# Moving half of the first layer's output projection beside the second attention, and the context rows behind the first feed-forward products

## Chip, cores, metric

One Trainium2 chip, one of its cores. The metric is the device time of one execution in microseconds (us). TensorE (PE) multiplies, VectorE (DVE) and ScalarE (ACT) do the elementwise work, SyncE (SP) issues the large loads from HBM, and all engines run their own instructions in the order in which they were laid down, waiting on one another through semaphores.

## The reference

Two blocks of two layers each on 256 token rows of width 1024. Only the first layer of the first block matters here; its "even mixer" treats the 256 latent rows and 256 context rows together:

```python
h_l = modulate(x_l, sh1_l, sc1_l); h_c = modulate(x_c, sh1_c, sc1_c)
# ya: neighbourhood attention, yb: differential attention, 512 columns each
y_l = concat([merge_heads(ya_l), merge_heads(rms_norm(yb_l, subln) * (1.0 - lam_init))]) @ w_out
x_l = x_l + g1_l * y_l                      # the same for the context rows
h2  = modulate(x_l, sh2_l, sc2_l)           # row norm, scale, shift
x_l = x_l + g2_l * conv_ffn(h2, w_up, conv_w, conv_b, w_down)
```

The six vectors sh1, sc1, g1, sh2, sc2, g2 of each layer come from one product of the conditioning vector with `w_ada` (1024 x 6144).

## The kernel before

Rows lie as four row tiles of 128 (two of the latent rows `xl`, two of context `xc`, together `xs`), each in two halves of 512 columns. Products in full precision are made of three: an operand is split into a rounded part and a remainder (`wh`, `wl` of a weight: ACT's cast in L359, DVE's subtraction in L360), and `mm3` (L381 to L384) adds high x high, high x low, low x high into a PSUM bank. A weight piece of 1 MB is loaded by SP into one of **three** staging tiles `ws` (`wtile`, L271 to L274, with `loads=3`), then split by `wload` into two of four `wh` and two of four `wl`. Loads are issued in program order, and each waits until its staging tile has been read.

The order of work around the change, in the code from L951:

- `weave` runs generators side by side, always the one that is furthest behind for its share. The second attention `da_att` (L909) goes over four row tiles `t`, and in each over four heads: scores (L879), row maximum on DVE (L921), exponential on ACT (L790), the difference of the two softmaxes (L926), four transposes (L781), the copy of these on ACT (L339), the product with the values (L785). A tail per row tile (L935 to L944: square on ACT, a sum and some fifteen tiny DVE instructions, one multiplication) makes `O[t][1]`.
- Beside it runs `ada` (L437) for three pairs: (0,2) gives g1 and sh2, (0,4) gives sc2 and g2, (1,0) belongs to the next layer. Each pair takes eight loads of 1 MB and, for each, four products straight from the staging tile (L445), then a turn of the result (copy, L454) and a small addition.
- Then the way out: `to_feature` (L714) transposes 128 columns of `O` for all four row tiles, `pairs_from` (L579) splits them; `gate` (L501) spreads g1 over 128 rows by products with a diagonal (L512 on DVE, L518 on PE); `lin_tok` (L632) multiplies with `w_out_e`, all four row tiles of one half of the columns at a time over eight pieces of 128 (`k`), into four banks `acc`; `add_gated` (L673) multiplies by the gate and adds to the row tile (L676, L677). The second half's products wait until all its weights are there and go row tile by row tile (`skew`).
- `modulate` (L561) makes the input of the feed-forward: `norm_rows` (squares in L533, a chain of tiny DVE instructions from L535, multiplication in L539), then per 128 columns two transposes (L550), scale and shift (L571 to L574), split (L575, L576). For the latent rows it runs before the last row tiles; for the context rows it is handed to `conv_ffn` as `begin` and woven with the first products of the latent rows (`stream`, 24 products of 256 columns for each of four results).

A scheduler reorders what `weave` and the code lay down, engine by engine, so the built order is finer than the code's.

Of the kernel before, what the change touches and what calls it, by code (L numbers as in the profile page):

```python
# [166 lines left out]
def run(g):  # L167
    for _ in g:
        pass
# [32 lines left out]
def body(tc, A, stop=None):  # L202
# [62 lines left out]
    def bank():  # L265
        return taken("w")
# [233 lines left out]

    def gate(layer, ch, stream, gb, tag="gate"):  # L501

# [5 lines left out]
        for h in range(2):  # L508
# [6 lines left out]
            yield 0.1  # L515
            ps = bank()
            for j in range(2):
# [195 lines left out]

    def to_feature(rows, cols):  # L714

        ps = bank()
        for i, r in enumerate(rows):
            pe.transpose(ps[:, i * 128:(i + 1) * 128], r[:, cols], ident)
        return ps
# [148 lines left out]
    def v_chunk(c0, res):  # L868
        yield from lin_tok(hT, T4, W, c0, 512, KT, collect(res, lambda: own("v")))
# [39 lines left out]
    def da_att(t):  # L909
# [5 lines left out]
        def unit(j):  # L915
# [13 lines left out]
            def second(P):  # L929
# [19 lines left out]
                 qk_chunk(1536, rtab[0], 0.125, gcol[:, 2:3], qB),  # L949
                 v_chunk(2560, vB)), 68))  # L950
    serve(acc=["a"], pt=["b"])  # L951
    weave((chain(*[da_att(t) for t in T4]), 36), (ada((0, 2), (0, 4), (1, 0)), 24))

    g1 = [[], []]
    gt = chain(*[gate(0, 2, i, g1[i], "v") for i in T2])
    banks(acc=4, w=4)
    oT = [[None] * 8, [None] * 8]
    out = [lin_tok(oT, T4, A["w_out_e"], c0, 512, KT, add_gated(xs, [g1[0], g1[0], g1[1], g1[1]], c0, 512), c0 > 0)
           for c0 in (0, 512)]
    for f in range(8):  # L960
        ps = to_feature([O[t][f // 4] for t in T4], slice((f % 4) * 128, (f % 4) * 128 + 128))
        oT[0][f], oT[1][f] = pairs_from(ps, 512, subln if f >= 4 else None)
        next(gt)
        if f > 1:
            next(out[0])
    run(out[0])
    for _ in range(3):
        next(out[1])
    prs = [pair_tiles(512, "qk") for _ in range(KT)]
    hT = ([p[0] for p in prs], [p[1] for p in prs])  # L970
    run(modulate(prs, (xl, 0, 0), mod[0, 3], mod[0, 4], range(KT)))
    run(out[1])

    def conv_ffn(layer, hT, T, xs, beside=(), begin=None, then=None, gate_tag="gate", act_tags=("act",)):
# [34 lines left out]
        for lo, hi in ((0, 12), (12, NHT)):  # L1009
            acts = []  # L1010
            for f0 in range(lo, hi, 2):
                ww = [wcols(A["w_up"][layer], b + f0 * 128) for b in (0, HID)]
                outs = [pair_tiles(T, act_tags[min((f0 - lo + f) // 4, len(act_tags) - 1)]) for f in T2]
                if f0 == 0 and begin:
                    weave((stream(ww, outs, 0), 10), (begin, 8))
                    run(stream(ww, outs, 256))
# [12 lines left out]
            for c0 in (0, 512):  # L1029
# [5 lines left out]
    conv_ffn(0, hT, 512, xs, ((1, 2),),  # L1035
             modulate(prs, (xc, 1, 256), mod[0, 3], mod[0, 4], range(KT)), None, "oa", ("v", "h"))

# [1130 lines left out]
```

## Time and profile before

| | us |
|---|---|
| median of 3 runs | 2036.98 |
| their range | 2036.53 to 2042.06 |
| the profiled execution, its own time | 2039.93 |
| its span | 2038.1 |
| PE busy in it | 1949.2 (96%) |
| DVE, ACT busy | 1375.5 (67%), 1015.2 (50%) |

The stretch of the change runs from the first scores of the second attention (240 us) to the end of the first four results of the feed-forward for the latent rows (408 us): 168 of the 2038 us. Idle time of PE counts there, and time in which PE runs at the lower of its two clock levels; the profile gives the granted clock as a share of full speed, and half is the lower level.

### The profile page before, as it was taken

How to read it: one execution, taken by the hardware profiler on the slowest of the kernel's cores; microseconds unless marked ns; L12 is line 12 of the kernel's file. 1: busy time of each engine (PE TensorE's matmuls, PEld its weight loads, DVE VectorE, ACT ScalarE, POOL GpSimd, SP SyncE). 2: the span in 40 equal slices, each digit the busy share in tenths (PEclk: the TensorE clock that was granted, in tenths of full speed). 3: DMA queues.
4: the chain of work that ended last, by engine and by line, in shares of the span. 5: the costliest groups of instructions: out<-in, count | busy, mean ns of one | idle time of the engine just before them, and what ended most of it. 6: DMA issues, size and time to landing. Idle time of an engine off the chain costs nothing.

```text
span 2038.1 us, 27898 instructions
## 1 busy us (share of the span) xinstructions
PE 1949.2 (96%) x10697; PEld 1579.4 (77%) x10697; DVE 1375.5 (67%) x2559; ACT 1015.2 (50%) x1662; POOL 31.7 (2%) x65
## 2 busy tenths in 40 slices
PE   7999997899999999998999998899999999999998
PEld 2777545787888888667989866698989788888886
DVE  4546355655445549755767677675767799999897
ACT  4433443433323326254645555454544577777775
POOL 1000000000000000000000200000000000000000
PEclk9999998899999999998999998999999999999999
DMA  9222195136322233444554453445565399999996
GB/s 329 85 93 82 75 318 172 63 124 207 104 89 98 74 117 120 150 146 145 167 200 161 142 171 98 128 165 187 166 193 184 132 356 325 339 332 335 330 334 222
DMA packets 220841, 369.67 MB, mean 181 GB/s; under 512 B 7328, under 2 KB 117516, under 8 KB 215580
## 3 DMA queue, kind: packets, MB, share of 16 engines
q1 hardware_dynamic: 218252, 362.06, 52.6%
q0 software_dynamic: 2448, 5.75, 1.0%
q8 instruction: 86, 1.41, 0.3%
q14 instruction: 55, 0.45, 0.1%
HBM read 366.73 MB, written 1.05 MB: 180 GB/s over the span
## 4 chain that ended last, share of the span: by engine, by line
PE 88%; DVE 5%; ACT 3%; DMA 2%; issue 1%; SPq 0%; ACTq 0%; DVEq 0%
PE w L382 16%; PE w L383 16%; PE w L384 16%; PE acc L384 6%; PE acc L382 6%; PE acc L383 6%; PE ob L785 2%; PE w L879 2%; PE a L382 2%; PE a L384 1%; PE a L383 1%; PE b L382 1%; PE b L384 1%; PE b L383 1%; PE a L445 1%
## 5 line engine op out<-in xcount | busy, mean ns | idle before, releaser
L360 DVE TENSOR_TENSOR wl<-ws,wh 128x1024 fp32r<-128x1024 f32 (+3 forms) x600 | 691.5, 1171 | 251.2 <-ACT wh L359 245.6
L359 ACT CAST wh<-ws 128x1024 fp32r<-128x1024 f32 (+3 forms) x600 | 594.5, 1008 | 377.0 <-PE acc L384 157.3
L382 PE MATMUL w<-h,wh 128*128 128x256 f32 x992 | 283.8, 287 | 2.8 <-DVE raw L1791 1.4
L383 PE MATMUL w<-h,wh 128*128 128x256 f32 x992 | 283.6, 287 | 0.0
L384 PE MATMUL w<-h,wl 128*128 128x256 f32 x992 | 282.2, 285 | 0.5 <-DVE wl L360 0.5
L382 PEld LDWEIGHTS w<-h,wh 128*128 128x128 f32 x992 | 192.5, 194 | 9.7 <-DVE raw L1791 1.6
L384 PEld LDWEIGHTS w<-h,wl 128*128 128x128 f32 x992 | 192.4, 194 | 1.5 <-DVE wl L360 0.7
L383 PEld LDWEIGHTS w<-h,wh 128*128 128x128 f32 x992 | 192.6, 194 | 1.1 <-issue 0.7
L382 PE MATMUL w<-qk,wh 128*128 128x512 f32 (+1 forms) x384 | 146.0, 380 | 0.9 <-ACT t L574 0.9
L383 PE MATMUL w<-qk,wh 128*128 128x512 f32 (+1 forms) x384 | 143.8, 375 | 2.1 <-DVE qk L576 2.1
L383 PE MATMUL w<-wl,h 128*128 128x512 f32 (+1 forms) x384 | 145.1, 378 | 0.7 <-DVE wl L378 0.6
L382 PE MATMUL w<-wh,h 128*128 128x512 f32 (+1 forms) x384 | 144.4, 377 | 0.1
L384 PE MATMUL w<-qk,wl 128*128 128x512 f32 (+1 forms) x384 | 144.3, 376 | 0.0
L384 PE MATMUL w<-wh,h 128*128 128x512 f32 (+1 forms) x384 | 143.7, 374 | 0.0
L382 PE MATMUL acc<-wh,h 128*128 128x512 f32 x272 | 110.0, 405 | 4.0 <-ACT h L583 4.0
L384 PE MATMUL acc<-wh,h 128*128 128x512 f32 x272 | 108.2, 398 | 2.6 <-DVE h L584 2.6
L383 PE MATMUL acc<-wl,h 128*128 128x512 f32 x272 | 107.6, 396 | 0.0
L382 PEld LDWEIGHTS w<-qk,wh 128*128 128x128 f32 x384 | 73.0, 190 | 20.3 <-issue 3.4
L790 ACT ACTIVATE P<-w,s 128x512 f32<-128x512 f32 (+1 forms) x80 | 48.3, 605 | 78.8 <-DVE s L921 28.9
L383 PEld LDWEIGHTS w<-qk,wh 128*128 128x128 f32 x384 | 73.1, 190 | 15.8 <-DVE qk L576 2.6
L383 PEld LDWEIGHTS w<-wl,h 128*128 128x128 f32 x384 | 72.4, 189 | 15.7 <-DVE wl L360 3.8
L384 PEld LDWEIGHTS w<-qk,wl 128*128 128x128 f32 x384 | 73.0, 190 | 13.7
(508 smaller groups left out, 3570.5 us busy)
## 6 DMA issues: line engine op xcount, KB each, us to landing
ws<-in_w_up_dram SPq DMA_DIRECT2D x44, 1024.0 KB, 5.1
ws<-in_w_ada_dram SPq DMA_DIRECT2D x40, 1024.0 KB, 5.0
ws<-in_m_gate_dram SPq DMA_DIRECT2D x32, 1024.0 KB, 6.5
ws<-in_m_up_dram SPq DMA_DIRECT2D x32, 1024.0 KB, 7.8
ws<-in_m_down_dram SPq DMA_DIRECT2D x32, 1024.0 KB, 6.8
ws<-in_w_down_dram SPq DMA_DIRECT2D x20, 1024.0 KB, 5.1
ws<-in_w_in_e_dram SPq DMA_DIRECT2D x12, 1024.0 KB, 5.2
ws<-in_od_w_in_dram SPq DMA_DIRECT2D x12, 1024.0 KB, 5.6
```

Source lines behind the costliest of these rows:

```text
L359: act.copy(wh, ws[:, k:k + e])
L360: split = vec.tensor_tensor(wl, ws[:, k:k + e], wh.bitcast(F32), op=OP.subtract)
L382: pe.matmul(out, lhsT=ah, rhs=bh, start=start, stop=False)
L383: pe.matmul(out, lhsT=ah, rhs=bl, start=False, stop=False)
L384: pe.matmul(out, lhsT=al, rhs=bh, start=False, stop=stop)
L445: pe.matmul(acc[32 * j:32 * j + 32, :], lhsT=cs[:, k, :], rhs=w, start=start, stop=stop)
L785: pe.matmul(ps, lhsT=pts[:, j * 128:(j + 1) * 128], rhs=vs[j][:, vcols], start=first and j == 0, stop=j == n // 128 - 1)
L790: act.activation(P[:, :n], S, AF.Exp, bias=nmax, scale=scale, accum_out=total)
L879: pe.matmul(S[:, :n], lhsT=q[po:po + 64, t * 128:(t + 1) * 128], rhs=k[po:po + 64, 512 - n:512], start=True, stop=True)
```

## The change

- `beside_da` replaces the bare `ada` calls beside the second attention. It runs ada (0,2), then transposes the first four column pieces of the first attention's output (`way_out`), makes all gates, then multiplies them with the upper half of `w_out_e` (`out_rows`: four `k`, one row tile and one half of the columns at a time, added to the rows at once): four row tiles with columns 0 to 511, ada (0,4), four row tiles with columns 512 to 1023, ada (1,0). Inside the last ada it loads the lower half of `w_out_e` (`Wo`).
- After the attention come the four other transposes, the two latent row tiles, `modulate` of the latent rows, the two context row tiles.
- Context's `norm_rows` moves into `begin` (`begin_context`), whose weight in the weave grows from 8 to 12.
- PSUM keeps its division of the attention (`a`, `b` two banks each, `w` three, `ob` one) up to the end of the feed-forward, instead of four `acc` and four `w`.

Every row of `xs` is now added to twice per half of the columns (16 pairs of L676 and L677 instead of 8); matmuls, loads and their sizes are the same.

```diff
+    def out_weights(k0, c0):
+        return wload(A["w_out_e"][k0 * 128:(k0 + 4) * 128, c0:c0 + 512].rearrange("(a p) n -> p a n", p=128), 4, 512)
+    def out_rows(t, k0, c0, wb):
+        ps = bank_a()
+        for k in range(4):
+            c = slice(t * 128, (t + 1) * 128)
+            mm3(ps, oT[0][k0 + k][:, c], oT[1][k0 + k][:, c], wb[k][0], wb[k][1], k == 0, k == 3)
+        add_gated(xs, [g1[0], g1[0], g1[1], g1[1]], c0, 512)(t, t, ps)
+    def beside_da():
+        yield from ada((0, 2))
+        for f in range(4):
+            way_out(f, bank_a)
+            yield 0.5
+        for i in T2:
+            yield from gate(0, 2, i, g1[i], "v", bank_a)
+        for c0 in (0, 512):
+            wb = out_weights(0, c0)
+            for t in T4:
+                out_rows(t, 0, c0, wb)
+                yield 2.7
+            if c0 == 0:
+                yield from ada((0, 4))
+        last = ada((1, 0))
+        for i in range(9):
+            if i in (4, 6):
+                Wo.append(out_weights(4, 512 * (i == 6)))
+            yield next(last)
+        yield from last
+
     serve(acc=["a"], pt=["b"])
-    weave((chain(*[da_att(t) for t in T4]), 36), (ada((0, 2), (0, 4), (1, 0)), 24))
...
-    banks(acc=4, w=4)
...
-    for f in range(8):
-        ps = to_feature([O[t][f // 4] for t in T4], slice((f % 4) * 128, (f % 4) * 128 + 128))
-        oT[0][f], oT[1][f] = pairs_from(ps, 512, subln if f >= 4 else None)
-        next(gt)
-        if f > 1:
-            next(out[0])
-    run(out[0])
-    for _ in range(3):
-        next(out[1])
+    weave((chain(*[da_att(t) for t in T4]), 36), (beside_da(), 51))
+    serve(acc=["a", "b"], w=["w", "w", "w", "ob"], pt=["w"])
+    for f in range(4, 8):
+        way_out(f, bank)
     prs = [pair_tiles(512, "qk") for _ in range(KT)]
     hT = ([p[0] for p in prs], [p[1] for p in prs])
-    run(modulate(prs, (xl, 0, 0), mod[0, 3], mod[0, 4], range(KT)))
-    run(out[1])
+    for i, ts in enumerate((T2, (2, 3))):
+        for c0 in (0, 512):
+            for t in ts:
+                out_rows(t, 4, c0, Wo[c0 // 512])
+        if i == 0:
+            run(modulate(prs, (xl, 0, 0), mod[0, 3], mod[0, 4], range(KT)))
+    def begin_context():
+        xn = norm_rows(xc)
+        yield 4
+        yield from modulate(prs, (xn, 1, 256), mod[0, 3], mod[0, 4], range(KT))
```

How the built order moves, at three places. First SP's queue at the end of the attention (`ada` loads, `w_out_e` loads, then the first of `w_up`), before:

```order
L273 DMA ws_638_2595<-in_w_ada_dram 128x2048
L273 DMA ws_648_2624<-in_w_ada_dram 128x2048
L273 DMA ws_693_2755<-in_w_out_e_dram 128x4x512
L273 DMA ws_720_2871<-in_w_out_e_dram 128x4x512
L273 DMA ws_738_2959<-in_w_out_e_dram 128x4x512
L273 DMA ws_743_2969<-in_w_out_e_dram 128x4x512
L273 DMA ws_792_3189<-in_w_up_dram 128x8x256
```

and after:

```order
L273 DMA ws_695_2812<-in_w_ada_dram 128x2048
L273 DMA ws_703_2834<-in_w_out_e_dram 128x4x512
L273 DMA ws_708_2844<-in_w_ada_dram 128x2048
L273 DMA ws_711_2857<-in_w_ada_dram 128x2048
L273 DMA ws_712_2863<-in_w_out_e_dram 128x4x512
L273 DMA ws_717_2873<-in_w_ada_dram 128x2048
L273 DMA ws_725_2895<-in_w_ada_dram 128x2048
L273 DMA ws_807_3217<-in_w_up_dram 128x8x256
```

The `w_out_e` loads now stand between those of ada; the two before these (one for each half of the columns) stand after the eighth and the sixteenth ada load. On PE the products of the last two loads before (`a` is ada's bank, then its turn L454 and the first transposes of the way out):

```order
L785 MATMUL ob_620_2554<-v_446_1989,pt_663_2674 128x128
L445 MATMUL a_558_2358<-ws_638_2595,cs_95 32x512 x4
L785 MATMUL ob_620_2554<-v_447_1991,pt_663_2674 128x128
L445 MATMUL a_558_2358<-ws_648_2624,cs_95 32x512 x4
L454 MATMUL w_661_2662<-ident_89,t_651_2637 128x128 x4
L718 MATMUL w_672_2707<-ident_89,oa_258_1285 128x128
```

and after:

```order
L785 MATMUL ob_672_2751<-v_447_1991,pt_730_2913 128x128
L445 MATMUL a_682_2770<-ws_708_2844,cs_95 32x512 x4
L445 MATMUL a_682_2770<-ws_711_2857,cs_95 32x512 x4
L445 MATMUL a_682_2770<-ws_717_2873,cs_95 32x512 x4
L445 MATMUL a_682_2770<-ws_725_2895,cs_95 32x512 x4
L454 MATMUL w_738_2942<-ident_89,t_728_2908 128x128 x4
L718 MATMUL w_739_2951<-ident_89,h_551_2327 128x128
```

The last four ada products now stand alone behind all of the attention's. Second, DVE where the gates are made (`dg` diagonals for the gates, `v` the gates themselves, `s` and `P` the attention's softmax and tail, `wl` remainders of `w_out_e`), before:

```order
L512 TENSOR_TENSOR dg_678_2722<-ident_89,s_676_2717 128x512
L940 TENSOR_TENSOR s_665_2679<-s_665_2679,s_664_2678 128x4
L512 TENSOR_TENSOR dg_687_2747<-ident_89,gh_675_2716 128x512
L392 TENSOR_SCALAR s_667_2686<-s_665_2679 128x4
L512 TENSOR_TENSOR dg_688_2749<-ident_89,s_676_2717 128x512
L393 TENSOR_SCALAR s_668_2687<-s_667_2686 128x4
L360 TENSOR_TENSOR wl_695_2758<-ws_693_2755,wh_694_2757 128x1024
```

and after:

```order
L512 TENSOR_TENSOR dg_517_2206<-ident_89,gh_515_2202 128x512
L926 SCALAR_TENSOR_TENSOR P_493_2141<-P_495_2145,s_496_2147,P_493_2141 128x512
L512 TENSOR_TENSOR dg_518_2208<-ident_89,s_516_2203 128x512
L921 TENSOR_REDUCE s_523_2219<-w_521_2215 128x1
L343 COPY v_520_2213<-a_519_2210 128x512
L921 TENSOR_REDUCE s_525_2223<-w_522_2217 128x1
L512 TENSOR_TENSOR dg_528_2231<-ident_89,gh_515_2202 128x512
L512 TENSOR_TENSOR dg_529_2233<-ident_89,s_516_2203 128x512
L924 RECIPROCAL s_527_2227<-s_456_2013 128x1
L360 TENSOR_TENSOR wl_534_2243<-ws_532_2240,wh_533_2242 128x1024
```

All eight diagonals, with the attention's work between them, now stand ahead of the remainder that the first row tile needs; before, four of them did. Third, DVE where the context rows end and their norm begins (`xc` the rows, `s_822` and `s_807` the sums of squares, `qk` the latent rows' last pieces of `modulate`), before:

```order
L676 TENSOR_TENSOR t_790_3157<-acc_736_2957,v_729_2905 128x512
L576 TENSOR_TENSOR qk_765_3072<-t_789_3153,qk_764_3071 128x256
L677 TENSOR_TENSOR xc01_86<-xc01_86,t_790_3157 128x512
L676 TENSOR_TENSOR t_791_3184<-acc_737_2958,v_729_2905 128x512
L677 TENSOR_TENSOR xc11_88<-xc11_88,t_791_3184 128x512
L535 TENSOR_TENSOR s_807_3238<-s_807_3238 128x2
```

and after:

```order
L676 TENSOR_TENSOR t_800_3164<-a_799_3151,v_520_2213 128x512
L576 TENSOR_TENSOR qk_766_3002<-t_798_3147,qk_765_3001 128x256
L677 TENSOR_TENSOR xc00_85<-xc00_85,t_800_3164 128x512
L676 TENSOR_TENSOR t_802_3180<-b_801_3167,v_520_2213 128x512
L676 TENSOR_TENSOR t_804_3196<-a_803_3183,v_531_2238 128x512
L677 TENSOR_TENSOR xc10_87<-xc10_87,t_802_3180 128x512
L677 TENSOR_TENSOR xc01_86<-xc01_86,t_804_3196 128x512
L676 TENSOR_TENSOR t_806_3212<-b_805_3199,v_531_2238 128x512
L677 TENSOR_TENSOR xc11_88<-xc11_88,t_806_3212 128x512
L535 TENSOR_TENSOR s_822_3266<-s_822_3266 128x2
```

All four context pieces are now added behind the last piece of the latent rows, where two were before.

## Rows read from the trace of the kernel before

**Rows 1.** The page's first part: busy time of each engine in the span.

```profile
PE 1949.2 (96%) x10697; PEld 1579.4 (77%) x10697; DVE 1375.5 (67%) x2559; ACT 1015.2 (50%) x1662; POOL 31.7 (2%) x65
```

**Rows 2.** Stretches: us, busy PE, PEld, DVE, ACT, POOL, then PEclk, DMA share, GB/s.

```profile
240.00:408.00 168.00, 144.44 (x802) 93.47 (x801) 101.86 (x282) 67.53 (x155) 0.00 (x0) 0.94 0.54 190
...
250.00:260.00 10.00, 10.00 (x56) 4.26 (x48) 5.15 (x13) 3.75 (x10) 0.00 (x0) 1.00 0.99 366
...
280.00:290.00 10.00, 7.17 (x56) 3.23 (x54) 2.29 (x6) 2.78 (x8) 0.00 (x0) 1.00 0.89 311
...
320.00:330.00 10.00, 3.40 (x10) 2.17 (x11) 9.83 (x25) 3.98 (x6) 0.00 (x0) 0.72 0.80 283
...
380.00:390.00 10.00, 4.63 (x28) 3.74 (x26) 8.90 (x22) 5.58 (x13) 0.00 (x0) 0.79 0.63 210
390.00:400.00 10.00, 8.00 (x49) 7.64 (x50) 5.18 (x16) 3.09 (x7) 0.00 (x0) 0.70 0.00 1
```

**Rows 3.** PE in order of time: start, us, line, tile, count, idle before.

```profile
286.73 1.06 PE L445 MATMUL a<-ws,cs 128*32 128x512 f32 x8 [0.97 <-DMA ws<-in_w_ada_dram]
...
315.93 1.06 PE L445 MATMUL a<-ws,cs 128*32 128x512 f32 x8 [1.03 <-DMA ws<-in_w_ada_dram]
...
324.83 0.79 PE L382 MATMUL acc<-wh,h 128*128 128x512 f32 x1 [4.00 <-ACT h L583]
...
328.65 0.80 PE L384 MATMUL acc<-wh,h 128*128 128x512 f32 x1 [2.60 <-DVE h L584]
...
334.96 0.40 PE L383 MATMUL acc<-wl,h 128*128 128x512 f32 x1
335.19 0.40 PE L384 MATMUL acc<-wh,h 128*128 128x512 f32 x1
```

**Rows 4.** PE in order of time around the context rows' norm.

```profile
384.19 0.39 PE L383 MATMUL w<-qk,wh 128*128 128x256 f32 x1 [1.32 <-DVE qk L576]
...
391.57 1.21 PE L550 MATMUL w<-ident,raw 128*128 128x128 f32 x4 [4.87 <-DVE raw L539]
...
398.02 0.39 PE L382 MATMUL w<-qk,wh 128*128 128x256 f32 x1 [0.44 <-ACT t L574]
...
407.90 0.38 PE L383 MATMUL w<-qk,wh 128*128 128x256 f32 x1
```

**Rows 5.** The tile `in_w_ada_dram`, 236 to 330 us: issues, and time to landing.

```profile
L273 SPq DMA_DIRECT2D ws<-in_w_ada_dram x21: 327/328/331, 244.3 to 308.0; - x21
...
DMA to landing us min/median/max: 4.8/6.9/7.9
```

**Rows 6.** The chain of waits: start, us, engine, tile, line (x2 = one score).

```profile
240.07 1.05 PE w L879 x2
...
249.53 1.00 PE a L445 x8
...
255.08 1.09 PE ob L785 x8
...
297.18 0.62 PE w L879 x2
```

**Rows 7.** Groups by shape, 318 to 410 us: count, busy us, mean ns.

```profile
L360 DVE TENSOR_TENSOR wl<-ws,wh 128x1024 fp32r<-128x1024 f32 x12 | 14.6, 1223 | 7.8 <-ACT wh L359 7.8
...
L359 ACT CAST wh<-ws 128x1024 fp32r<-128x1024 f32 x13 | 13.4, 1046 | 14.4 <-PE acc L384 11.4 <-DMA ws<-in_w_out_e_dram 2.2 <-PE w L383 0.7
```

**Rows 8.** DVE in order of time: start, us; instructions that follow without a wait.

```profile
327.91 0.68 DVE L584 TENSOR_TENSOR h<-w,h 128x512 fp32r<-128x512 f32 x1
328.51 0.68 DVE L512 TENSOR_TENSOR dg<-ident,gh 128x512 fp32r<-128x512 f32 x1
```

**Rows 9.** DVE in order of time: the last attention tail, the context's norm.

```profile
318.18 0.69 DVE L938 TENSOR_REDUCE s<-t 128x4 f32<-128x512 f32 x1 [6.42 <-ACT t L937]
...
388.57 0.16 DVE L535 TENSOR_TENSOR s<-s 128x2 f32<-128x2 f32 x1 [0.79 <-ACT raw L533]
...
390.94 1.67 DVE L539 TENSOR_SCALAR raw<-xc,s 128x512 f32<-128x512 f32 x4
```

More of the change, by code (lines that the diff above doesn't have):

```diff
@@ L499, in ada, with gate @@
         finish(*late)
-    def gate(layer, ch, stream, gb, tag="gate"):
+    def gate(layer, ch, stream, gb, tag="gate", new=bank):
         m = mod[layer, ch][:, :, stream]
@@ L515, in gate @@
             yield 0.1
-            ps = bank()
+            ps = new()
             for j in range(2):
@@ L712, in rope_pairs, with to_feature @@
         vec.tensor_tensor(rv, rv, av, op=OP.add)
-    def to_feature(rows, cols):
-        ps = bank()
+    def to_feature(rows, cols, new=bank):
+        ps = new()
         for i, r in enumerate(rows):
@@ L950, in body @@
                  v_chunk(2560, vB)), 68))
-    serve(acc=["a"], pt=["b"])
-    weave((chain(*[da_att(t) for t in T4]), 36), (ada((0, 2), (0, 4), (1, 0)), 24))
-    g1 = [[], []]
-    gt = chain(*[gate(0, 2, i, g1[i], "v") for i in T2])
-    banks(acc=4, w=4)
-    oT = [[None] * 8, [None] * 8]
-    out = [lin_tok(oT, T4, A["w_out_e"], c0, 512, KT, add_gated(xs, [g1[0], g1[0], g1[1], g1[1]], c0, 512), c0 > 0)
-           for c0 in (0, 512)]
-    for f in range(8):
-        ps = to_feature([O[t][f // 4] for t in T4], slice((f % 4) * 128, (f % 4) * 128 + 128))
-        oT[0][f], oT[1][f] = pairs_from(ps, 512, subln if f >= 4 else None)
-        next(gt)
-        if f > 1:
-            next(out[0])
@@ L966, in body, with way_out @@
-    run(out[0])
-    for _ in range(3):
-        next(out[1])
+    g1 = [[], []]
+    oT = [[None] * 8, [None] * 8]
+    Wo = []
+    def way_out(f, new):
+        ps = to_feature([O[t][f // 4] for t in T4], slice((f % 4) * 128, (f % 4) * 128 + 128), new)
+        oT[0][f], oT[1][f] = pairs_from(ps, 512, subln if f >= 4 else None)
+    def out_weights(k0, c0):
[6 more added lines that the diff above has]
+        add_gated(xs, [g1[0], g1[0], g1[1], g1[1]], c0, 512)(t, t, ps)
@@ L1014, in conv_ffn @@
                 if f0 == 0 and begin:
-                    weave((stream(ww, outs, 0), 10), (begin, 8))
+                    weave((stream(ww, outs, 0), 10), (begin, 12))
                     run(stream(ww, outs, 256))
@@ L1035, in body @@
     conv_ffn(0, hT, 512, xs, ((1, 2),),
-             modulate(prs, (xc, 1, 256), mod[0, 3], mod[0, 4], range(KT)), None, "oa", ("v", "h"))
+             begin_context(), None, "oa", ("v", "h"))
     if stop == "L0":
```

## The prediction

> **What bounds the kernel now.** I read the page's busy shares first: PE works in 96% of the span, no other engine in more than 67% [rows 1]. So only time that PE loses can be won. I then read the stretches from 240 to 408 us, the one in which the change moves work, and PE in order of time there. In these 168 us PE is busy for 144.4, at a mean granted clock of 0.94 [rows 2], so it is idle for 23.6 us, and at the lower level (1.2 of 2.4 GHz) the clock costs some 6 us more: the stretches that start at 320, 380 and 390 us show 0.72, 0.79 and 0.70 [rows 2]. The losses are of three kinds. Up to 317 us ada's loads keep the DMA engines at a share of 0.89 to 0.99, and late in it PE waits for them [rows 2, 3]. Behind the attention PE waits 4.00 and 2.60 us for the first pairs, and runs slowly up to about 334; at 334.96 it is at full speed again, 0.23 us from product to product [rows 3]. Then it waits 1.32 and 4.87 us for the end of the latent rows' `modulate` and for the context rows' norm [rows 4]. The most that can be won is thus about 29 us, 1.4%.
>
> **Prices.** A score of 512 columns takes 1.05 us and one of 256 columns 0.62, eight ada products (one load) 1.00, a set of value products 1.09 [rows 6]; a row tile of `out_rows` is 12 products of 0.23 = 2.76 [rows 3], a result of `stream` 24 products of half that length, 2.8. The split of a weight piece is two casts of 1.05 on ACT and two subtractions of 1.22 on DVE [rows 7]; DVE's instructions of 512 columns, the diagonals among them, are 0.68 long and follow each other in 0.60 [rows 8]. A load takes 4.8 us to land at best, 6.9 in the median [rows 5]; with the queue full it is 1.05 MB / 366 GB/s = 2.87 us from one to the next [rows 2].
>
> **The change, stretch by stretch.** PE's matmuls are the same, so I lay the new orders out over the old prices. Each stretch ends at the point that I name, and its length is PE's work there or the wait that ends later.
>
> (a) 240 us to the end of the first ada set. Three loads are there, five more follow from 244.3 on [rows 5], each when a staging tile is free, so the eighth lands at about 259.3, and its products end at 260.4. PE has about 18 of these 20.4 us to do; the transposes of the first four column pieces fit in, and wait for nothing else.
>
> (b) To the end of the first four row tiles: 27.6 us. The gates now lie on the path. DVE has eight diagonals, two evacuations and five attention instructions ahead of the first remainder, 15 x 0.60 plus 1.4 for tiny ones, and then the remainder's 1.22: with ada's turn (1.3) and 0.5 for waits on PE's scores this is 13.4 us until the second product of the first row tile can run. PE has 10 to 12 us of scores and gate products in that time. Then come 4 x 2.76 and 3.2 of attention.
>
> (c) The second ada set: 19.5 us. Three loads are waiting, five are issued as the products free the tiles; PE's work (8 x 1.00, four scores at 1.05, four sets of values, transposes) is 18.4, and the loads at 2.87 come out about 1 us later.
>
> (d) To the end of the second four row tiles: 22.3 us. The `w_out_e` piece is issued behind the five loads, lands when the set ends, and its split ends 2 us after PE has done three scores; then 17.4 of PE's work.
>
> (e) The third ada set: 26 us, against 14.3 of PE's work. Three of its eight ada loads have landed; the other five and two of `w_out_e` are still to come: seven loads that nothing could issue earlier, since only three staging tiles exist and PE read none of them during (d). The first lands 1.5 + 4.8 after the start, six more at 2.87 each, then 1.06 of products: 24.6. One of them comes about 1.4 later, since its tile is freed by a split that stands behind the last softmax on ACT and DVE: 26. The DMA engines meanwhile stand idle in (b) and (d), for about 20 and 10 us; that is where the time of (e) comes from.
>
> (f) To the first product of the lower half: 6.4 us. ACT's square of the last tail stands behind ada's last copy, so the tail still starts when ada ends: copy and square 1.2, the sum 0.69 [rows 9], 14 tiny instructions at 0.2 = 2.8, the multiplication 0.69, transpose and cast 0.9. Before, the same took 7.8 us from 316.99 to the first product, and 11.7 to the steady run at 328.65 [rows 3], because DVE did four remainders and the diagonals in between.
>
> (g) The eight row tiles of the lower half and the latent rows' 16 transposes: 22.1 + 1.8, plus 2.8 for the low clock after the idle time (as before: 5.5 us of steady work at half speed, 328.65 to about 334) and 0.4: 27.0.
>
> (h) To the context rows' first transpose: 12.4 us. PE has 5.6 us of products (48). DVE first ends the latent rows' last piece, whose scale on ACT waits for two casts that need the last `wh`, then the context rows' seven additions (7 x 0.65), ACT squares, the tiny chain takes 390.94 - 388.57 = 2.4 [rows 9]. PE is idle for about 6.8 us, where it waited 4.87 [rows 4]: the wait that the change means to hide is not hidden, since the first two results only last 5.6 us and the next two stand behind the transposes.
>
> (i) To the end of the latent rows' four results: 10.4 us, two results (5.6), 16 transposes (1.8), low clock (2.2), two waits like the 0.44 for a bank [rows 4].
>
> The sum: 20.4 + 27.6 + 19.5 + 22.3 + 26 + 6.4 + 27.0 + 12.4 + 10.4 = 172.0, against 168 (240 to 407.9 [rows 2, 4]). Behind it nothing moves. So the change costs 4 us: 2043.9 against the profiled execution's own 2039.93, and 2041 against the median of 2036.98, which lies 3 us below that execution. About 0.3% (6.1 us) is what a measurement of this kernel can tell from no change.
>
> Bounds of what the trace does not show. (e) is 24.6 us if no load waits for a split; at the pace of all 21 issues, (308.0 - 244.3) / 20 = 3.19 [rows 5], it is 28, and at the 311 GB/s of 280 to 290 us (3.37 a load [rows 2]) 29. I take the 366 GB/s row, which is the one with a full queue. (b) is 25 if DVE's diagonals slip between the softmax, and 30 if PE's sparse work there costs the clock. (d) is 21 to 25 for the same two reasons, (h) is 9 if DVE adds the context rows ahead of the last piece, 14 if ACT is late. PSUM's new division and the doubled additions lie beside PE's row tiles, which take four times as long, except in (h), where they are counted.
>
> Of the clock the trace shows both: between 280 and 290 us PE is busy for 7.17 of 10 and the granted clock stays at 1.00; after the 4 us of idle time behind 320 it has fallen [rows 2, 3]. The Trainium skill (TensorE: Matmul & The Clock Gate, "HAM oscillation") warns of matmul batches that each wait for a DMA, since each batch then runs cold; (e) is such a loop. By that rule its last products would take 2 us instead of 1; by the row at 280 us they would not.
>
> **Rivals.** *PE stays the bound* (faster). If loads land in time for (c) to (e), because tiles come free in the gaps of PE's order, (e) is its 14.3 us of work, and the sum falls by 11.7 to 160.3: 2029. For it speaks that PE's idle time before was small while loads took 3.2 us each; against it that the last four ada products stand in a row behind everything. It decides if the fourth load of (e) is issued before (d) ends. The Trainium skill (Perfetto Trace Analysis, "Optimization Strategy") advises to interleave regimes with different limits, which would give this result; the old stretch does so already.
>
> *Loads are as slow as before, and the clock falls* (slower). If loads take 3.2 to 3.4 us each, the pace of all issues and of the row at 280 us [rows 2, 5], (a), (c) and (e) grow by 1.5, 2 and 2 to 3, and with PE busy for half of (b) and (e) the first row tiles of each half run at the lower level, 2 us each: 6 to 10 on top of 4, 2047 to 2051. It decides from 3.2 us a load on.
>
> *The change hides what it says* (faster by a little): the context norm ends before the first two results do; (h) is 5.6 and (i) loses its 2.2: 163, or 2032. DVE's order speaks against it.
>
> **Chances.** The sum as worked, within 6 us of no change: 0.45. PE stays the bound: 0.10. The hidden norm: 0.10, half of it (with a shorter (e)) beyond 0.3%. The slow loads and the clock: 0.35, taken as beyond 0.3% since some of it comes on top of the 4 us already. So faster 0.15, same 0.50, slower 0.35. The likeliest is 2041; the range from 2031 to 2051 takes in the bounds of (b), (d), (e) and (h) and most of the slow case, and leaves out PE as the bound.
>
> **What would show it.** In the changed profile: DMA at a low share for some 20 us in the first row tiles and 10 in the second; L445 waiting for `ws` behind the last value products; the stretch from the last score to the first lower product over 15 us; DVE's diagonals ahead of L360 with PE waiting; L550 waiting for `raw` about 7 us. I am wrong if the DMA share stays above 0.8 through the attention, or if PE's order has other gaps than these.

## The result

The changed kernel takes 2057.86 us (2050.36 to 2063.15) where the kernel before takes 2036.76: slower by a factor of 1.0094 (1.0077 to 1.011). A second set of runs gave 2058.72 beside 2039.19, 1.0099 (1.0078 to 1.012). The prediction was 2041, its range ended at 2051. Its nine runs lie in two groups, 2050.4 to 2052.9 (two) and 2057.0 to 2063.2 (seven); the first profile is of a run of 2050.36, a second one, called "again" below, of 2056.99, and what lies between the two is shown there.

First the profile of 2050.36, against the profiled execution of before, 2039.93. Stretches (us, busy time of PE, PEld, DVE, ACT, POOL, then granted clock, DMA share, GB/s): of the kernel before from 240 us to the start of the context rows' first feed-forward result, then of the changed kernel to the same instruction, and 10-us stretches of it.

```profile
240.00:405.18 165.18, 141.62 (x780) 90.83 (x779) 99.46 (x276) 65.85 (x151) 0.00 (x0) 0.94 0.55 193
```

```profile
240.00:416.20 176.20, 147.09 (x779) 90.94 (x778) 110.86 (x292) 65.57 (x152) 0.00 (x0) 0.92 0.50 181
...
270.00:280.00 10.00, 9.75 (x41) 6.70 (x42) 8.85 (x17) 3.80 (x10) 0.00 (x0) 1.00 0.31 107
280.00:290.00 10.00, 10.00 (x49) 6.80 (x48) 8.84 (x28) 3.23 (x7) 0.00 (x0) 1.00 0.00 0
...
320.00:330.00 10.00, 10.00 (x47) 6.71 (x46) 8.43 (x32) 3.12 (x12) 0.00 (x0) 1.00 0.01 2
...
350.00:360.00 10.00, 3.87 (x16) 0.40 (x16) 2.36 (x2) 2.04 (x3) 0.00 (x0) 0.57 0.98 374
360.00:370.00 10.00, 7.71 (x31) 6.68 (x32) 6.55 (x24) 3.46 (x6) 0.00 (x0) 0.57 0.87 273
...
400.00:410.00 10.00, 5.01 (x23) 4.49 (x24) 7.08 (x24) 3.93 (x11) 0.00 (x0) 0.66 0.00 1
```

The stretch is 11.0 us longer, and behind it the two kernels stay about that far apart, 10.4 us at the end (spans of 2048.5 and 2038.1). PE does the same matmuls; it is idle for 29.1 us instead of 23.6, and its busy time grows by 5.5 us. The lower clock makes some 4 of these at most, by an estimate from the two rows (8% of 176.2 us at a mean of 0.92, less 6% of 165.2 at 0.94); where the rest comes from is not shown. The DMA engines rest while PE does row tiles (0.00 and 0.01) and are full when PE waits (350 to 360 us: PE busy for 3.87 us, DMA share 0.98). Before, the deepest dip stood at 320 us, where DVE was busy for 9.83 [rows 2]; now it is at 350 us, and DVE is busy for 2.36.

PE in order of time, the instructions that end the stretches (a) to (i) of the prediction (start, us, line, tile, count, idle time before and what ended it):

```profile
259.73 1.06 PE L445 MATMUL a<-ws,cs 128*32 128x512 f32 x8 [1.90 <-DMA ws<-in_w_ada_dram]
...
274.45 0.40 PE L383 MATMUL a<-wl,h 128*128 128x512 f32 x1
...
287.60 0.39 PE L384 MATMUL a<-wh,h 128*128 128x512 f32 x1
...
307.80 1.06 PE L445 MATMUL a<-ws,cs 128*32 128x512 f32 x8 [1.34 <-DMA ws<-in_w_ada_dram]
...
330.50 0.39 PE L384 MATMUL a<-wh,h 128*128 128x512 f32 x1
...
355.44 1.94 PE L445 MATMUL a<-ws,cs 128*32 128x512 f32 x8 [5.76 <-DMA ws<-in_w_ada_dram]
357.95 1.93 PE L445 MATMUL a<-ws,cs 128*32 128x512 f32 x8 [0.57 <-DMA ws<-in_w_ada_dram]
...
365.32 0.90 PE L718 MATMUL w<-ident,h 128*128 128x128 f32 x3 [1.70 <-DVE h L944]
...
366.73 0.78 PE L382 MATMUL a<-wh,h 128*128 128x512 f32 x1
...
404.76 0.78 PE L550 MATMUL w<-ident,raw 128*128 128x128 f32 x2 [6.79 <-DVE raw L539]
...
416.20 0.38 PE L382 MATMUL w<-qk,wh 128*128 128x256 f32 x1 [0.80 <-DVE t L572]
```

Each stretch, predicted and measured in us: (a) 20.4, 20.8; (b) 27.6, 27.0; (c) 19.5, 21.0; (d) 22.3, 21.9; (e) 26, 29.1; (f) 6.4, 6.9; (g) 27.0, 25.4, to the first feed-forward product at 392.09; (h) 12.4, 12.7; (i) 10.4 to 414.57, 9.8. Their sum, 174.6, is 2.6 us above the 172.0 of the prediction; then come transposes and a wait of 0.80, 1.6 us together, to the 416.20 of the last row. The rest of the difference is no term but the other side of the subtraction, told below.

**The two groups.** The second profile differs from the first where ada's first set ends. The same instructions there, PE in order of time:

```profile
261.85 1.60 PE L445 MATMUL a<-ws,cs 128*32 128x512 f32 x8 [3.02 <-DMA ws<-in_w_ada_dram]
264.14 1.11 PE L454 MATMUL w<-ident,t 128*128 128x128 f32 x4 [0.69 <-ACT t L339]
265.19 2.08 PE L879 MATMUL w<-qk,qk 64*128 64x512 f32 x4
...
296.02 0.39 PE L384 MATMUL a<-wh,h 128*128 128x512 f32 x1
```

PE waits 1.1 us longer for the eighth load. SP issued it at the same place in both, 10.0 us after the first of the five that follow the three already there; from its issue to its products it is 5.75 us in the first profile and 6.87 in the second, so it was the transfer that took longer. From then on scores take 2.07 us instead of 1.12 and the gates' products 0.79 instead of 0.50. The stretch 262 to 280 us, of the first profile and then of the second:

```profile
262.00:280.00 18.00, 17.02 (x63) 9.43 (x62) 16.65 (x38) 8.11 (x17) 0.00 (x0) 1.00 0.45 176
```

```profile
262.00:280.00 18.00, 17.07 (x41) 7.04 (x36) 9.86 (x25) 6.58 (x13) 0.00 (x0) 0.53 0.36 143
```

PE is as busy in both, but at 0.53 of its clock it does 41 instructions instead of 63. Stretch (b) takes 32.8 us instead of 27.0, and the first feed-forward product starts at 398.55 instead of 392.09. The mean granted clock of a whole run, which is known for all nine, parts the groups too: 0.981 and 0.982 in the lower one, 0.974 to 0.979 in the upper one. Most runs are of this kind, so the median is.

### The profile page after: what moved, and what is told of

It reads as the page before. It is cut to its first block, busy times and chain, and to the rows that moved or that the text cites. A ratio compares the mean times of both kernels' runs of the same rounds, so it can differ in the third digit from the quotient of the medians.

```text
span 2048.5 us, 27908 instructions
## 1 busy us (share of the span) xinstructions
PE 1953.9 (95%) x10697; PEld 1579.2 (77%) x10697; DVE 1386.6 (68%) x2575; ACT 1014.8 (50%) x1662; POOL 31.6 (2%) x65
## 3 DMA queue, kind: packets, MB, share of 16 engines
q0 software_dynamic: 2448, 5.75, 1.0%
## 5 line engine op out<-in xcount | busy, mean ns | idle before, releaser
L382 PE MATMUL w<-qk,wh 128*128 128x512 f32 (+1 forms) x296 | 111.5, 378 | 1.0 <-DVE t L572 0.8
L384 PE MATMUL w<-qk,wl 128*128 128x512 f32 (+1 forms) x296 | 110.4, 373 | 0.0
L383 PE MATMUL w<-qk,wh 128*128 128x512 f32 (+1 forms) x296 | 109.9, 371 | 0.0
L382 PE MATMUL a<-wh,h 128*128 128x512 f32 (+2 forms) x272 | 107.2, 397 | 2.1 <-ACT wh L359 1.9
L383 PE MATMUL a<-wl,h 128*128 128x512 f32 (+2 forms) x272 | 105.4, 388 | 0.6 <-DVE wl L360 0.5
L384 PE MATMUL a<-wh,h 128*128 128x512 f32 (+2 forms) x272 | 105.2, 387 | 0.4 <-DVE h L576 0.4
L382 PE MATMUL b<-wh,h 128*128 128x512 f32 (+3 forms) x220 | 84.9, 386 | 0.7 <-ACT h L586 0.4
L383 PE MATMUL b<-wl,h 128*128 128x512 f32 (+3 forms) x220 | 84.4, 384 | 0.0
L384 PE MATMUL b<-wh,h 128*128 128x512 f32 (+3 forms) x220 | 84.3, 385 | 0.0
```

Of the source, the lines that this page charges most:

```text
L382: pe.matmul(out, lhsT=ah, rhs=bh, start=start, stop=False)
L383: pe.matmul(out, lhsT=ah, rhs=bl, start=False, stop=False)
L384: pe.matmul(out, lhsT=al, rhs=bh, start=False, stop=stop)
```

## Experiments

Medians are given beside those of the kernel before on the same chip.

**again** (2058.72 beside 2039.19): the changed kernel as it is.

> The changed kernel once more, for a second profile and more times. Its four runs fell in two groups, 2050 to 2053 and 2063 us. Theory 1 (the groups differ by TensorE's clock): the profile of a run near 2063 has one or more stretches at half the clock that the first profile (2050) lacks, worth 10 to 13 us together, and the same waits elsewhere; a run near 2051 repeats the first profile. Theory 2 (the groups differ by when loads land): the profile near 2063 has longer waits of L445 for its loads at the same clock.

Theory 1 as to the kind, with something of theory 2 at its start: the clock differs, from 262 us on, behind a load that is 1.1 us late. The size is 6 to 7 us for this run. Of the runs of 2060 to 2063 there is no profile; their mean clock is lower still (0.974 to 0.976, where this run has 0.978), so they hold more time at the lower level, but where is not known.

**spread** (2046.80, 2037.87 to 2052.91, beside 2039.19): ada's products between the row tiles.

```
+        rest = ada((0, 4), (1, 0))
         for c0 in (0, 512):
             wb = out_weights(0, c0)
             for t in T4:
-                out_rows(t, 0, c0, wb)
+                out_rows(t, 0, c0, wb, bank_p)
                 yield 2.7
-            if c0 == 0:
-                yield from ada((0, 4))
-        last = ada((1, 0))
...
+                yield next(rest)
+                yield next(rest)
...
+        yield from rest
```

> The sixteen ada products of (0, 4) and (1, 0) stand two by two between the first eight row tiles, which evacuate from the other PSUM tag; nothing else is changed. Theory 1 (the extra time is that of loads which three staging tiles hold back while PE does row tiles in a block): the DMA engines no longer stand idle in the row tiles, the waits of L445 fall from 10 us to under 4, and the 99 us from the end of the first ada set to the end of the last one become 85 to 89: 2036 to 2042 us. Theory 2 (PE's own order and DVE bound the stretch, the loads are hidden anyway): within 4 us of the changed kernel's lower group, 2047 to 2052.

Five runs lie at 2037.9 to 2041.2, where theory 1 put them (mean clock 0.983 to 0.985), and seven at 2046 to 2053 (0.977 to 0.980). The one profile is of the second kind, with the clock at half from 263 to 286 us; the 99 us of theory 1 are 96.0 in it, with that fall inside. Its stretches behind the fall:

```profile
300.00:310.00 10.00, 10.00 (x55) 5.92 (x53) 4.87 (x10) 2.14 (x5) 0.00 (x0) 1.00 0.60 223
310.00:320.00 10.00, 10.00 (x55) 5.42 (x54) 6.97 (x12) 5.70 (x12) 0.00 (x0) 1.00 0.75 279
320.00:330.00 10.00, 10.00 (x56) 6.03 (x58) 7.53 (x25) 2.92 (x9) 0.00 (x0) 1.00 0.69 258
```

Loads now run beside row tiles, and PE has no gap. So the order of ada's sets as blocks between blocks of row tiles costs some 12 us in the lower group (2039.6 in the middle, where the changed kernel has 2050.4 and 2052.9) and some 8 in the upper one (2050.8 against again's 2058.7). The row tiles also moved to the other PSUM tag, and the loads of `w_out_e` moved with them; no run parts these from the order.

**warm** (2083.39) and **warm2** (2059.68, 2057.34 to 2064.66, beside 2037.16): products with zeros in the two waits, added to ada's accumulator (they change nothing in it) and to a free bank.

```
+            for i in range(warm.get(k, 0)):
+                pe.matmul(acc[0:32, :], lhsT=z32, rhs=O[0][0], start=False, stop=False)
...
-        last = ada((1, 0))
+        last = ada((1, 0), warm={5: 2, 6: 20, 7: 3})
...
```

> The changed kernel with products that multiply zeros and add them to the same accumulator, 2, 20 and 3 of them before the last three ada products, and 24 more into a free bank while PE waits for the context rows' norm: PE waits as long but isn't idle. Theory 1 (of the 10.9 us some 6 are clock, lost behind those two waits, and the upper group of runs is more of it): the granted clock stays at 1.00 through both, the time is 2044 to 2047 in all runs, with no upper group. Theory 2 (the clock falls for other reasons, or the waits are all of it): 2049 to 2052 with the upper group still there.

> As warm, but with 6 zero products before the last but one of ada's loads and 7 before the context rows' transposes. In warm a zero product took 0.87 us, since all of them go to the same 32 rows of the accumulator (39 records in 16.90 us), where eight ada products over four groups of rows take 1.00: 25 and 24 of them made PE work 21.9 and 19.9 us, far longer than the waits they stand in, so the kernel's time said nothing. 6 and 7 of them are 5.2 and 6.1 us, within waits of 5.8 and 6.8. Theory 1 (the clock lost behind the two waits is worth 5 to 6 us): 1.00 from 350 to 372 and from 398 to 415 us, 2045 to 2047 in the lower group, 2052 in the upper one, which belongs to the gates. Theory 2 (that clock costs nothing on the path): 2050 and 2058.

warm missed both theories: a zero product is 3.5 times as long as I took it for (PE in order of time, two rows of eight-product sets and zero products):

```profile
344.39 1.92 PE L447 MATMUL a<-ws,cs 128*32 128x512 f32 x14
...
360.62 16.90 PE L445 MATMUL a<-oa,z 128*32 128x512 f32 x39
```

warm2, with six and seven of them (warm={6: 6}), missed theory 1's times too; they lie where theory 2 has the upper group. In its profile the zero products end in time for the loads:

```profile
359.55 5.31 PE L445 MATMUL a<-oa,z 128*32 128x512 f32 x12
367.03 1.06 PE L447 MATMUL a<-ws,cs 128*32 128x512 f32 x8 [2.17 <-DMA ws<-in_w_ada_dram]
369.59 1.94 PE L447 MATMUL a<-ws,cs 128*32 128x512 f32 x8 [1.49 <-DMA ws<-in_w_ada_dram]
```

One of the two ada products is back at 1.06 us, the other is not, and the loads come as late as before. From the last score to the first feed-forward product it is 50.2 us (352.4 to 402.6) against 49.5 in again. So the clock lost in (e) costs little by itself, since the loads end last there. Behind the second wait theory 1 held: the clock stays at 1.00 from 398 to 415 us, and from the first feed-forward product to the context rows' first result it is 22.7 us (402.60 to 425.25) instead of 24.0 in again (398.55 to 422.51). That clock is worth 1.3 us.

**out_only** (2059.09, 2055.04 to 2063.60, beside 2039.19): the way out as changed, the context rows' norm as before, PSUM divided as before behind the attention.

```
-    serve(acc=["a", "b"], w=["w", "w", "w", "ob"], pt=["w"])
+    banks(acc=4, w=4)
...
-                    weave((stream(ww, outs, 0), 10), (begin, 12))
+                    weave((stream(ww, outs, 0), 10), (begin, 8))
...
-             begin_context(), None, "oa", ("v", "h"))
+             modulate(prs, (xc, 1, 256), mod[0, 3], mod[0, 4], range(KT)), None, "oa", ("v", "h"))
```

> The way out as changed, but the context rows' norm as before (outside the feed-forward's first products, begin and its weight of 8), and PSUM divided as before behind the attention. Theory 1 (the way out makes the whole loss, the moved norm is worth half a us either way): 2050 to 2053 in the lower group. Theory 2 (PE's 6.8 us of idle time before L550 is the moved norm's fault): 2043 to 2046.

**ctx_only** (2037.44, 2032.79 to 2041.89, beside 2038.53; 0.9987, 0.9972 to 1.0003): the moved norm alone, on the kernel before.

> The kernel before with the last part of the change alone: the context rows' norm and modulate stand inside the feed-forward's first products, with a weight of 12. out_only, the change without that part (and with PSUM divided as before), gave 2055 in its lower group where the changed kernel gives 2050 to 2053. Theory 1 (the moved norm gains 2 to 4 us, as that difference says): 2033 to 2035 beside 2037. Theory 2 (PE only waits elsewhere, 6.8 us instead of 4.9): 2037 to 2039.

The whole loss is in the way out, as theory 1 of out_only says, though its lowest run, 2055.0, is 2 us above that theory's figure. The moved norm alone can't be told from nothing, which is theory 2's time, but not its reason: in ctx_only's profile L550 waits 3.84 us, not 6.8. In out_only's, where the norm stands as before, it waits 7.56. So the longer wait of the changed kernel (6.79) came with the way out and not with the norm's new place.

**gates_fill** (2048.94, 2046.47 to 2051.59, beside 2037.16): ada's second set between the steps of the gates; the row tiles stay in blocks.

```
-        for i in T2:
-            yield from gate(0, 2, i, g1[i], "v", bank_a)
+        between = ada((0, 4))
+        for i in T2:
+            for c in gate(0, 2, i, g1[i], "v", bank_p):
+                yield c
+                yield next(between)
+        yield from between
...
-            if c0 == 0:
-                yield from ada((0, 4))
```

> The changed kernel with the eight products of ada's second set put one by one between the steps of the two gates, so that PE has work while DVE makes the diagonals; the row tiles stay in blocks. In the second profile of the changed kernel the granted clock was 0.5 from 262 to 279 us, behind 3.02 us of waiting for the first set's last load and through the gates, where the first profile had 1.00. Theory 1 (PE's sparse work between the gates brings the clock down there, and that is the upper group): the clock stays at 1.00 from 262 to 280 us, no upper group, 2045 to 2051 in all runs. Theory 2 (the wait for the last load before it is enough): the low stretch is there in some runs, 2050 and 2058 as before.

None of the five runs is in the upper group, and the times are in theory 1's range, but for one at 2051.6. The clock did fall behind the wait for the eighth load, as theory 2 has it, but not for long: 0.84 in the stretch 262 to 280 us, with 80 of PE's instructions where again had 41.

```profile
262.00:280.00 18.00, 17.29 (x80) 6.15 (x74) 11.78 (x31) 6.34 (x16) 0.00 (x0) 0.84 0.82 301
```

**fill** (2039.33, 2033.50 to 2041.67, beside 2037.16; 1.0007, 0.9998 to 1.0016): both, ada's products between the gates' steps and then one behind each row tile.

> Both: eight ada products between the gates' steps, the other eight between the row tiles. Spread alone gave 2038 to 2041 us in runs with the clock at 0.984, 2046 to 2053 in runs with 0.978, and its profile had 24 us at half the clock from 263 us on. Theory 1 (loads and the gates' clock are the two causes, and they add up): 2033 to 2039 us in nearly all runs, at or below the kernel before. Theory 2 (the clock falls behind the first set whatever stands there): two groups again, as spread.

Theory 1: the two causes add up, 2058 comes down to 2039 with no upper group, though six of the eleven runs lie above 2039, and the rest can't be told from the kernel before. First the gates' stretch of its profile (no fall, although PE had waited 2.79 us for the eighth load), then, PE in order of time, what it waits for behind the last attention:

```profile
262.00:280.00 18.00, 17.59 (x91) 7.03 (x92) 13.86 (x36) 8.05 (x21) 0.00 (x0) 1.00 0.93 345
```

```profile
352.45 0.90 PE L718 MATMUL w<-ident,h 128*128 128x128 f32 x3 [4.97 <-DVE h L944]
```

**later** (2051.68, 2048.16 to 2059.56, beside 2038.53): ada's third set out of the attention, into the feed-forward.

```
-        last = ada((1, 0))
-        for i in range(9):
-            if i in (4, 6):
-                Wo.append(out_weights(4, 512 * (i == 6)))
-            yield next(last)
-        yield from last
+        Wo.append(out_weights(4, 0))
+        yield 3
+        Wo.append(out_weights(4, 512))
...
-    conv_ffn(0, hT, 512, xs, ((1, 2),),
+    conv_ffn(0, hT, 512, xs, ((1, 0), (1, 2)),
```

> The changed kernel with ada's third set moved out of the attention into the first layer's feed-forward, ahead of (1, 2); the rest as changed, the gates before their diagonals with nothing beside them. Theory 1 (the third set's 29 us hold 14 us of PE's work, the rest is loads that came too late): some 19 us leave the stretch and 8 come back in the feed-forward, 2040 to 2043 in the lower group; the upper group, 2047 to 2050, remains, since it belongs to the gates. Theory 2 (another wait takes its place behind the last tail): 2048 and more.

All nine times are theory 2's, 2048 and more, again in two groups: five at 2048.2 to 2051.7, and four at 2054.9 to 2059.6, where the profile was taken. Theory 1 had the place right and the size wrong. From the last score to the first lower product it is 13.4 us (350.2 to 363.6) instead of 25.0 in again (349.0 to 374.0): 11.6 us, not 19, because the last attention has its own chain of waits, which the loads had covered. The feed-forward takes 7.5 us more (its casts lie 9.0 us behind those of the kernel before at its start, 16.5 further on). PE behind the last score, with nothing left beside the attention:

```profile
348.58 2.20 PE L879 MATMUL w<-qk,qk 64*128 64x256 f32 x4
...
362.21 0.90 PE L718 MATMUL w<-ident,h 128*128 128x128 f32 x3 [4.97 <-DVE h L944]
```

**blater** (2034.87, 2033.08 to 2036.21, beside 2037.16; 0.9988, 0.9979 to 0.9997): the same move on the kernel before (the attention with 16 beside it instead of 24).

> The kernel before with ada's third set, (1, 0), moved out of the attention into the first layer's feed-forward, ahead of (1, 2); two products a feature there instead of one or two. Theory 1 (ada's loads hold up the attention, here too: PE waits 3 us and more for them late in it): 8 products of 1.00 and some 4 to 6 us of waits leave the stretch, 8 come back in the feed-forward, 2030 to 2035. Theory 2 (the waits come from what stands around them, or the feed-forward's own loads are now late): 2037 to 2045.

At the edge of theory 1: 2.3 us less, small but outside the interval.

**fill_later** (2042.25, beside 2038.53) and **fill_later_ctx** (2039.27): ada's second set between the gates' steps and the third in the feed-forward; then the norm one result later in the feed-forward's first products (yield 9 instead of 4, weight 17 instead of 12).

> All three: ada's second set between the gates' steps, its third set in the feed-forward, the way out and the context rows' norm as changed. fill gave 2033 to 2042 and the kernel before with the third set moved 2035. Theory 1 (gates' clock, late loads and the third set's place are the causes, and with them gone the change does what it says): 2025 to 2032. Theory 2 (what is left, the last tail and the context rows' norm, costs as much as the kernel before had there): 2033 to 2037.

> fill_later with the context rows' norm one result later among the feed-forward's first products (its first step counts 9 instead of 4, the weight 17 instead of 12): PE has 2.8 us more to do while DVE adds the context rows, and waits 4 us instead of 6.8. Theory 1: 2 to 4 us below fill_later. Theory 2 (the two results left have nothing to run beside, DVE is the bound there): the same as fill_later within 1 us.

fill_later missed both theories, and it is no better than fill: with both sets gone from the last attention the clock falls there (0.57 from 330 to 340 us, 0.66 from 340 to 350), and ada's eight products come back in the feed-forward. The median of fill_later_ctx is 3.0 us lower, as its theory 1 says, but not shown to be so for its reason: L550 waits 4.02 us in its profile and had waited 4.09 in that of fill_later already, and the profiled runs (2039.51 and 2038.20) lie the other way round.

**pace42** (2051.95, 2047.82 to 2052.54, beside 2037.29): the changed kernel with the work beside the attention held back, so that PE has two scores more ahead of ada's last loads.

```
-    weave((chain(*[da_att(t) for t in T4]), 36), (beside_da(), 51))
+    weave((chain(*[da_att(t) for t in T4]), 36), (beside_da(), 42))
```

> The changed kernel with the work beside the attention counted 42 instead of 51, so that the attention runs further ahead: two scores more stand before the last products of ada's first set, where PE waited 1.90 us in the profile with the clock at 1.00 behind it and 2.47 to 3.13 in those with half the clock, and two fewer behind it. Theory 1 (the wait for the eighth load tips the clock, the gates only keep it there): the wait is under 1 us, the clock stays at 1.00 from 262 to 280 us in all runs, no upper group: 2048 to 2053; the third set, which is now further behind, may add some us. Theory 2 (PE's thin work between the gates is enough by itself): half the clock from some 265 us on in some or all runs, 2057 and more.

Theory 1 in all six times and in the one profile. The eighth load's products start without a wait, and the clock stays up through the same gates, though PE is busy for less of the stretch than in any of the others:

```profile
262.01 1.06 PE L445 MATMUL a<-ws,cs 128*32 128x512 f32 x8
```

```profile
262.00:280.00 18.00, 15.46 (x64) 8.67 (x65) 15.46 (x34) 8.51 (x18) 0.00 (x0) 1.00 0.51 172
```

The third set, now further behind, waits 2.53, 4.28 and 4.27 us for its loads, so the time is still that of the lower group.

**blater_ctx** (2033.62, 2032.16 to 2036.23, beside 2037.29; 0.9981, 0.9972 to 0.9989): blater with the moved norm.

> The kernel before with ada's third set in the feed-forward (alone 2034.9, before beside it 2037.2) and the context rows' norm inside the feed-forward's first products (alone 2037.4, before beside it 2038.5): the one part of the change that did not lose, on the version that gained. Theory 1 (they lie 40 us apart and add up): 3 to 4 us below the kernel before. Theory 2 (DVE has ada's evacuations and the norm in the same stretch): no better than the third set's move alone, 2 us below.

Theory 1: 3.7 us below the kernel before, the best of all, and it has none of the changed way out; 1.2 of these are the step from blater. In it L550 waits 2.20 us instead of 4.87 [rows 4]. That is not the moved norm's doing, since blater without it waits 1.50 there; ada's products from the feed-forward stand in that gap in both:

```profile
375.78 1.06 PE L445 MATMUL acc<-ws,cs 128*32 128x512 f32 x8 [0.58 <-DMA ws<-in_w_ada_dram]
379.04 1.11 PE L550 MATMUL w<-ident,raw 128*128 128x128 f32 x4 [2.20 <-DVE raw L539]
```

## Why the prediction missed

The median lies 16.9 us above 2041. Of these 6.5 lie between the sum's 2043.9 and the first profile's 2050.36: the subtraction and (e). Another 7.5 lie between that run and the median, most of it the clock in (b). The other 2.9 are the step from the profiled execution of before down to its median.

**Right:** Most of the loss of the lower group is where (e) put it. All the signs named came: DMA at rest in the first row tiles from 267 to 292 us, but for one load (share 0.31 and 0.00 above), and in the second for some 16 us, from 319 to 336, not 10 (0.01), L445 waiting 5.76 us behind the last value products, 24.4 us from the last score (342.3) to the first lower product, DVE's diagonals ahead of the first remainder (second product at 274.45, worked out as 273.8), L550 waiting 6.79 us (about 6.8). The rival in which PE stays the bound had its condition named, a load of (e) issued before (d) ends, and that did not happen; spread, which makes it happen, takes the 12 us off, in the lower group, that the rival gave it (11.7).

**The subtraction.** The step that failed first is the last one: 172.0 was laid against 168, which ends at 407.9 [rows 4]. That row, and the 408 us given for the stretch at the start, is the end of the context rows' first result, the fifth, while (i) ends with the latent rows' fourth. Before, that fourth ends at 404.83 and the fifth starts at 405.18:

```profile
404.71 0.28 PE L384 MATMUL w<-qk,wl 128*128 128x256 f32 x1
404.83 0.60 PE L550 MATMUL w<-ident,raw 128*128 128x128 f32 x4
405.18 0.36 PE L382 MATMUL w<-qk,wh 128*128 128x256 f32 x1
```

So the stretch to set against 172.0 was 164.8, and 3.1 us of work stood on one side alone. My own terms gave +7.2, that is 2047 for the profiled execution and 2044 for the median, instead of +4. With the 2.6 us by which the terms were short, and the 1.6 from the fourth to the fifth result where it had been 0.35, this makes the 11.0 measured.

**(e), 29.1 instead of 26.** I let the first of the seven loads be issued 1.5 us after (d); it was issued at 335.8, 5 us after, because PE's order has two scores, transposes and values ahead of the last products of the first ada load, which free the tile. The loads themselves were a little faster than said, 22.1 us from that issue to the last products, where 4.8 + 6 x 2.87 + 1.4 is 23.4, and one of them did wait for a split, as the prediction has it (the `w_out_e` issue at 347.87). DMA issues there (start, time to the end of the group, tile, count):

```profile
306.52 29.65 SPq L273 DMA_DIRECT2D ws<-in_w_ada_dram  x4
336.69 0.38 SPq L273 DMA_DIRECT2D ws<-in_w_out_e_dram  x1
338.33 4.08 SPq L273 DMA_DIRECT2D ws<-in_w_ada_dram  x2
347.87 0.38 SPq L273 DMA_DIRECT2D ws<-in_w_out_e_dram  x1
348.48 1.59 SPq L273 DMA_DIRECT2D ws<-in_w_ada_dram  x2
```

The fourth of the first group is (e)'s first load: 306.52 + 29.65 = 336.17, less the 0.33 that an issue takes [rows 5]. The last products also ran at half the clock, 1.93 us instead of 1.06. By the rule of the Trainium skill that the prediction weighed (TensorE: Matmul & The Clock Gate, "HAM oscillation") they would take 2 us, and the trace agrees; the row at 280 us, which I followed, had PE busy for 7 of 10 us and no gap like the 5.76 here.

In (g) the low clock was priced at 2.8 us; the granted clock is back at 1.00 from 369 us on, some 2 us into the row tiles, and (g) came out 1.6 us short, which by luck hid half of (e)'s miss.

**The clock in (b).** This is the larger miss, since it sets the median. I gave (b) a bound of 30 for it and, in the slow rival, 2 us for row tiles at the lower level; it was 32.8, and nearly all of it ahead of the row tiles, in scores and gate products. The thin work of the gates, as I had it, does not bring the fall by itself: pace42 has the same gates and no wait, and its clock stays up. What parts the profiles is PE's wait for the eighth load just ahead of the gates: (a) held it, 18 us of work in 20.4, and I priced it at its length alone. The profiles side by side, wait and then granted clock of 262 to 280 us: none and 1.00 (pace42), 1.89 and 1.00 (out_only), 1.90 and 1.00 (first profile), 2.03 and 0.62, falling later, at 266 us (warm2), 2.47 and 0.53 (later), 2.98 and 0.53 (spread), 3.02 and 0.53 (again), 3.13 and 0.53 (warm). With ada's products behind it the same wait costs less: 2.67 and 0.84 (gates_fill), 2.79 and 1.00 (fill), 2.23 and 1.00 (fill_later_ctx). Each is one profile, and pace42 also moves two scores from behind the wait to ahead of it; that thin work behind a wait keeps the clock down is argued from gates_fill and fill.

**The chances.** The slow rival was of the right kind, clock and late loads on top of the sum, and held 0.35. With the subtraction done rightly the sum alone would have been a forecast of slower, and the rival 2050 to 2054; its clock term, 2 us a half, should have been some 6 for the first half alone (32.8 against 27.0).

**Open.** Where the runs of 2060 to 2063 us lose the clock that again's 2057 does not, and why the eighth load lands later in some runs. And what is left of the change when both causes are gone: fill can't be told from the kernel before, so half the way out beside the attention gains nothing that shows, though its row tiles are covered; what PE waits for there is the last attention's own tail, 4.97 us for `h` of L944, the same in later, and 4.98 in fill_later and fill_later_ctx; no version was made to shorten it.

## What to carry to other kernels

Work with a queue of few staging tiles behind it is better spread between work that needs no loads; put in blocks, the loads stop in one block and are waited for in the next, and it is the order of the two, not the sum of either, that costs (here 12 us). A wait of 2 to 3 us on TensorE is not priced by its length alone: here one ahead of thin work cost 6 us more in clock. Move work ahead of it, or put dense work behind it. When a sum is laid against a measured stretch, both must end at the same instruction.

## What was not expected of the hardware

Products into different groups of 32 rows of the accumulator ran side by side, products into the same 32 rows one after another. Ada's products (two records each) go to four groups of 32 rows in turn, and 14 records take 1.92 us, 0.14 each; zero products of the same size, all to the first 32 rows, took 16.90 us for 39 records, 0.43 each, also at a granted clock of 1.00. Where PE's order parts one ada product from the other three of its load, it takes as long alone as the four do together: 0.97 us to the next instruction in the first profile, where a load's eight records take 1.00 [rows 6].

```profile
288.36 1.05 PE L445 MATMUL a<-ws,cs 128*32 128x512 f32 x2
```

The Trainium skill (TensorEngine Tiling (Array Packing), "Key Properties") says that such tiles operate independently and can run in parallel; these rows agree with it.

The clock did not follow the share of time in which PE was busy: 15.46 of 18 us at 1.00 in pace42, 17.07 of 18 at 0.53 in again. The wait ahead of the stretch told the two apart.
